# Making the low part of each fourth weight tile with an accumulating transfer in the weights-stationary projections

## The chip, the cores and the metric

One core of one Trainium2 chip runs the whole program. The metric is the device time of one execution in microseconds (us), as a median of several runs. The profile is one further execution, taken by the hardware profiler. Engines are named as the profile names them: PE is TensorE's matmul, PEld its weight load, ACT is ScalarE, DVE is VectorE, POOL is GpSimd, SP is the engine that issues the loads here.

## The reference

Two layers act on a residual stream `h` of 256 tokens by 2048 columns in float32. Each layer is `h += mixer(rms_norm(h))` and then `h += relu(rms_norm(h) @ up)^2 @ down`, with `up` 2048 by 8192 and `down` 8192 by 2048. The first mixer is a sparse attention (16 heads, 4 key heads, an indexer that keeps 64 of the keys), the second an mLSTM (8 heads). Nearly all arithmetic is the products of the stream with weights that are read once from memory, 2048 rows and 512 columns at a time.

## The kernel before, in words

To keep float32 accuracy, the kernel takes each float32 operand apart into a high part, which is its value in the type float32r, and a low part, the value minus the high part. A product of two operands is then three products of parts: high by high, high by low, low by high.

`weights()` (L138) supplies half a block of rows in two *weight tiles*. A weight tile is 256 rows by 512 columns, held as `[128, 2, 512]`, 512 KB. For each tile SP issues one load into a buffer of the tag `w` (five buffers); `split()` (L134) then makes `wh` on ACT (a copy that rounds, L135) and `wl = w - wh` on DVE (L136), each in one of four buffers. A call returns two tiles, and a projection of 2048 rows calls it four times, so it uses eight tiles.

There are two kinds of projection:

- `project()` (L151) has the activations stationary and the weights moving: twelve matmuls per weight tile, with 512 moving columns (L166 to L168). It serves the attention, the down matrix of the feed-forward part and most of the mLSTM.
- `project_t()` (L174) has the weights stationary and the activations moving. For each of the two blocks of 128 rows in a tile and each of four blocks of 128 columns it does one matmul with `wh` against the high and low parts of the activations together (512 moving columns, L191) and one with `wl` against the high part (256 moving columns, L193), so a tile is 16 matmuls. Its sums alternate between two groups of four PSUM banks, `acc` and `acx`. It serves the up matrix (32 calls, 16 in each layer) and the queries and keys of the mLSTM (4 calls).

After each `project_t()` of the feed-forward part, `evac_up()` (L457) empties the four banks: an ACT copy (L462), two DVE operations (L463, L464), and a split of the result into `hT` (L135 on ACT, L136 on DVE).

Order comes from the Tile framework: the program order, adjusted by its own simulated timeline at build time, with each engine executing its own list in order. A buffer is written again only when its readers are done. So the copy into `wh` for a tile waits for the last matmul that read the tile four earlier, and the load into `w` waits for the subtraction of the tile five earlier. POOL does masks at the start, two memsets per head group (L590), and four multiplications of the mLSTM's gate (L573); it issues no transfer.

Of the kernel before, what the change touches and what calls it, by code (L numbers as in the profile page):

```python
# [9 lines left out]
F32 = mybir.dt.float32  # L10
# [6 lines left out]
P = 128  # L17
# [20 lines left out]
def trunk_kernel(ctx: ExitStack, tc, x, norm_mix, norm_ffn, att_w_in, att_q_gain, att_k_gain,  # L38
# [18 lines left out]
        return f"{s}_{n[0]}"  # L57

    def pair(name):
        """The exact high and low parts of two blocks of 128 rows against all tokens."""  # L60
        return lp.tile([P, 2, 2, T], F32R, tag="pair", name=uid(name))

    def t2k(shape, dt=F32, name="t2k"):
# [23 lines left out]
        nc.tensor.transpose(pg[:, :32], g, ident[:32, :32])  # L87
        nc.vector.tensor_copy(gains[:, col:col + 32], pg[:, :32])

    # TensorE's clock comes up while the first loads run.  # L90
    warm = aux()
    for _ in range(8):
        nc.tensor.matmul(warm[:, :P], zero, zero, start=True, stop=True)
# [25 lines left out]
    nc.gpsimd.memset(one0[:, 1:2], 0.0)  # L119

    def rsqrt(a, cols):
        """1/sqrt of [P, cols] (in place of a tile's values), by Newton's method from a bit-level seed."""
        seed = small([P, cols], I32, "seed")
        y = small([P, cols], F32, "y")
        u = small([P, cols], F32, "u")
        nc.vector.tensor_scalar(seed, a.bitcast(I32), 1, None, op0=ALU.logical_shift_right)
        nc.vector.tensor_scalar(y.bitcast(I32), seed, -1.0, float(0x5F3759DF), op0=ALU.mult, op1=ALU.add)
        for _ in range(3):
            nc.vector.tensor_tensor(u, a, y, op=ALU.mult)
            nc.vector.scalar_tensor_tensor(u, u, -0.5, y, op0=ALU.mult, op1=ALU.mult)  # L130
            nc.vector.scalar_tensor_tensor(y, u, 1.5, y, op0=ALU.add, op1=ALU.mult)
        return y
# [2 lines left out]
        nc.scalar.copy(hi, src)  # L135
        nc.vector.tensor_tensor(lo, src, hi.bitcast(F32), op=ALU.subtract)  # L136

    def weights(src, k0, n0, width):  # L138
        """Rows k0.. (four blocks of 128) and columns n0..n0+width of a weight, as exact high and low parts."""
        parts = []  # L140
        for i in range(2):
            w = wp.tile([P, 2, 512], F32, tag="w", name=uid("w"), bufs=5)
            r0 = k0 + 256 * i
            nc.sync.dma_start(w[:, :, :width], src[r0:r0 + 256, n0:n0 + width].rearrange("(k p) f -> p k f", p=P))
            wh = wp.tile([P, 2, 512], F32R, tag="wh", name=uid("wh"), bufs=4)
            wl = wp.tile([P, 2, 512], F32R, tag="wl", name=uid("wl"), bufs=4)
            split(wh[:, :, :width], wl[:, :, :width], w[:, :, :width])
            parts.append((wh, wl))
        return parts

    def project(lhs, src, k0, n0, width, evac, before=None):  # L151
        """evac(m, psum): tokens of tile m against columns n0..n0+width. before(g) makes tiles 2g and 2g+1 of lhs."""
        acc = [pa.tile([P, 512], F32, tag="acc", name=uid("acc")) for _ in range(2)]
        nk = 2 * len(lhs)
        for g in range(nk // 4):
            if before is not None:
                before(g)
            for i, (wh, wl) in enumerate(weights(src, k0 + 512 * g, n0, width)):
                a = lhs[2 * g + i]
                for m in range(2):  # L160
                    ms = slice(m * P, (m + 1) * P)
                    o = acc[m][:, :width]
                    for j in range(2):
                        k = 4 * g + 2 * i + j
                        ah, al = a[:, 0, j, ms], a[:, 1, j, ms]
                        nc.tensor.matmul(o, ah, wh[:, j, :width], start=(k == 0), stop=False)  # L166
                        nc.tensor.matmul(o, ah, wl[:, j, :width], start=False, stop=False)  # L167
                        nc.tensor.matmul(o, al, wh[:, j, :width], start=False, stop=(k == nk - 1))  # L168
        for m in range(2):
            evac(m, acc[m][:, :width])  # L170
# [1 line left out]
    turn = [0]  # L172

    def project_t(lhs, src, n0, evac):  # L174
        """evac(b, psum): block b of 128 columns from n0 on, on the partitions, against all tokens; the product
        is the sum of the two halves of psum [128, 2, T]."""
        turn[0] ^= 1
        if turn[0]:
            acc = [pa.tile([P, 2, T], F32, tag="acc", name=uid("acc")) for _ in range(4)]
        else:  # L180
            acc = [px.tile([P, 2, T], F32, tag="aux", name=uid("acx")) for _ in range(4)]
        nk = 2 * len(lhs)
        for g in range(nk // 4):
            parts = weights(src, 512 * g, n0, 512)
            for kk in range(4):
                k = 4 * g + kk
                wh, wl = parts[kk // 2]
                a = lhs[k // 2]
                for j in range(4):
                    js = slice(j * P, (j + 1) * P)  # L190
                    nc.tensor.matmul(acc[j], wh[:, kk % 2, js], a[:, :, k % 2], start=(k == 0), stop=False,  # L191
                                     skip_group_check=True)
                    nc.tensor.matmul(acc[j][:, 1], wl[:, kk % 2, js], a[:, 0, k % 2], start=False,  # L193
                                     stop=(k == nk - 1), skip_group_check=True)
        for b in range(4):
            evac(b, acc[b])

    class Norm:
        """The stationary operand of a normed stream, without its tokens' factors; those come out of finish()."""

        def __init__(self, col):
            self.col = col
# [7 lines left out]
                                     accum_out=self.ss[:, m, c:c + 1])  # L210

        def chunk(self, c, squares=None):
            """squares: None for this chunk's own, True for those of all chunks, False for none."""
            for i in (2 * c, 2 * c + 1):
                p = aux()
                for j in range(2):
                    k = 2 * i + j
                    for m in range(2):
                        nc.tensor.transpose(p[:, j * T + m * P:j * T + (m + 1) * P],  # L219
                                            h[:, m, k * P:(k + 1) * P], ident)  # L220
                a = pair("xT")
                for j in range(2):
                    k = 2 * i + j
                    g = gains[:, self.col + k:self.col + k + 1]
                    src = p[:, j * T:(j + 1) * T]
                    nc.scalar.activation(a[:, 0, j], src, AF.Copy, scale=g)  # L226
                    nc.vector.scalar_tensor_tensor(a[:, 1, j], src, g, a[:, 0, j].bitcast(F32),
                                                   op0=ALU.mult, op1=ALU.subtract)
                self.lhs[i] = a
            for i in (range(4) if squares else (c,) if squares is None else ()):  # L230
                self.squares(i)
# [12 lines left out]
            return self  # L244

    def rope_cols(slab, v, heads, half, c0):
        """Turn the first 2*half columns of each head of v [P, 2, heads, d]."""
        rot = 2 * half
        shape = [P, 2, heads, rot]
        a = slab(shape, "ropa")  # L250
# [8 lines left out]
        nc.vector.tensor_tensor(v[:, :, :, :rot], a, b, op=ALU.add)  # L259

    def add_to_h(norm, r2=None):
        """Adds a product's columns to the stream, and hands them to the next norm."""

        def at(c):
            def evac(m, p):
# [8 lines left out]
        return at  # L274

    def slabs(pool, bufs):
        """Tiles of one phase: bufs by tag."""
        return lambda shape, name, tag=None: pool.tile(shape, F32, tag=tag or name, bufs=bufs[tag or name],
                                                       name=uid(name))

    # ---------------------------------------------------------------- attention
    def attention(nm, nxt, pool):
        slab = slabs(pool, {"v": 1, "kT": 1, "qT": 3, "hn": 3, "sq": 2, "ropa": 1, "ropb": 1, "lg": 5, "pT": 3, "sc": 4})
        lhs = nm.lhs
# [86 lines left out]
            bias.append(b)  # L371

        def heads_t(dst, gain):
            """evac of four heads of 128 columns: normed, turned and transposed into dst [P, 4, T]."""
            o = slab([P, 2, 4, DH], "hn")

            def evac(m, p):
# [71 lines left out]
            project(oT, w_ao, 0, 512 * c, 512, at(c))  # L449
        nxt.finish()  # L450

    # ---------------------------------------------------------------- feed-forward
    def ffn(nm, up, down, nxt, last=False):
        for q in range(4):
            hT = []
# [26 lines left out]
        if nxt is not None:  # L482
            nxt.finish()

    # ---------------------------------------------------------------- mLSTM
    def mlstm(nm, nxt, pool):
        slab = slabs(pool, {"go": 4, "mkT": 1, "mqT": 1, "mv": 2, "num": 2, "gT": 1, "row": 1, "et": 2, "pt": 2,
                            "mjunk": 2, "hs": 3})
# [4 lines left out]
        HD = MH * MV  # L493

        def put_o(m, c0, p, width):
            """sigmoid(o) times the heads' gain, for columns c0.. of o."""
            done = 0
            while done < width:
                c = c0 + done
# [17 lines left out]
        e = small([P, 2, MH], F32, "e")  # L517
        nc.vector.scalar_tensor_tensor(e, fg, -1.0, fg, op0=ALU.mult, op1=ALU.min)
        nc.scalar.activation(e, e, AF.Exp)
        # log(1 + e) as log(u) + (e - (u - 1)) / u, with u the rounded 1 + e.  # L520
        u = small([P, 2, MH], F32, "u1")
        ru = small([P, 2, MH], F32, "ru")
        nc.vector.tensor_scalar(u, e, 1.0, None, op0=ALU.add)
# [18 lines left out]
        nc.vector.tensor_tensor_scan(mm, cs, one0[:, 1:2].to_broadcast([MH, T]), 0.0, op0=ALU.max, op1=ALU.max)  # L542
        negm = slab([MH, T], "negm", "hs")
        nc.vector.scalar_tensor_tensor(negm, cum, -1.0, mm, op0=ALU.mult, op1=ALU.subtract)
        # Rows 0.. and 32.. of parts are the exact high and low parts of -mm; pick adds the two of one head.
        parts = pool.tile([40, T], F32R, tag="parts", bufs=1, name="parts")
        pick = cp.tile([40, MH], F32R, name="pick")
        nc.vector.tensor_tensor(pick, ident[:40, :MH], ident[:40, 32:32 + MH], op=ALU.add)
# [122 lines left out]


def _rope_table():
    """By position: [cos cos | -sin sin] of the attention's rotation, then the indexer's."""
    import numpy as np
    cols = []
    for rot in (RC, IC):
# [29 lines left out]
```

## Time and profile before

| what | value |
|---|---|
| median of 3 runs | 2126.35 us (2126.17 to 2127.8) |
| span of the profiled execution, first to last instruction | 2124.9 us |
| busy: PE, PEld | 2115.0 us, 1810.0 us |
| busy: DVE, ACT, POOL | 1242.6 us, 1010.1 us, 14.0 us |
| read from memory | 389.16 MB |

The profiled execution has no time of its own beside its span, which lies 1.45 us under the median of the runs. Busy times of different engines overlap, so they don't add up to the span; an engine that is busy for nearly all of it is the one whose work or waits the time is made of.

### The profile page before, as it was taken

Reading aid. Unit: us, or ns where it says so; the run is one execution under the profiler, and the core shown is the slowest. Engines: PE = TensorE matmul, PEld = TensorE weight load, DVE = VectorE, ACT = ScalarE, POOL = GpSimd, SP = SyncE. Lnnn points to the kernel's source line nnn. Section 1 sums busy time; section 2 is a strip of 40 time slices with the busy share of each in tenths; the row PEclk is TensorE's granted clock in tenths of the full one; section 3 lists DMA queues with packets and bytes.
Section 4 is the critical chain, followed back from the end, with each engine's and each line's share of the span. In section 5 each row is a group of like instructions: output and inputs, shape, how many; then the busy total and the mean of one; then the engine's idle time right before and its main releaser. Section 6 shows DMA issues by size and latency. Waiting matters only on the chain.

```text
span 2124.9 us, 27918 instructions
## 1 busy us (share of the span) xinstructions
PE 2115.0 (100%) x10748; PEld 1810.0 (85%) x10748; DVE 1242.6 (58%) x1866; ACT 1010.1 (48%) x1400; POOL 14.0 (1%) x20
## 2 busy tenths in 40 slices
PE   9999999999999999999999999999999999999999
PEld 8988888888888888888999888888888888888887
DVE  5697656645555565565654565656555555654654
ACT  6556554534443443444554554545434434443542
POOL 0000000000000000000011000000000000000000
PEclk9999999999999999999999999999999999999999
DMA  7665356656656656665566555466566666666664
GB/s 234 188 180 151 119 178 188 188 193 191 191 191 187 198 189 196 190 189 188 166 185 209 171 165 176 161 188 188 193 194 189 191 194 189 191 193 191 189 205 140
DMA packets 207926, 393.09 MB, mean 185 GB/s; under 512 B 12784, under 2 KB 29616, under 8 KB 207792
## 3 DMA queue, kind: packets, MB, share of 16 engines
q1 hardware_dynamic: 207744, 391.29, 60.4%
q8 instruction: 84, 1.38, 0.2%
q14 instruction: 50, 0.41, 0.1%
q10 hardware_dynamic: 48, 0.02, 0.0%
HBM read 389.16 MB, written 2.10 MB: 184 GB/s over the span
## 4 chain that ended last, share of the span: by engine, by line
PE 99%; ACT 0%; DMA 0%; DVE 0%; issue 0%; SPq 0%; DVEq 0%
PE acc L167 19%; PE acc L168 19%; PE acc L166 19%; PE acc L191 13%; PE acx L191 13%; PE acc L193 6%; PE acx L193 6%; PE aux L219 1%; PE aux L412 0%; PE aux L440 0%; PE aux L620 0%; PE aux L349 0%; DMA w<-in_att_w_in_dram 0%; PE aux L611 0%; PE aux L396 0%; PE aux L645 0%
## 5 line engine op out<-in xcount | busy, mean ns | idle before, releaser
L136 DVE TENSOR_TENSOR wl<-w,wh 128x1024 fp32r<-128x1024 f32 (+3 forms) x752 | 907.1, 1207 | 820.6 <-ACT wh L135 819.5
L135 ACT CAST wh<-w 128x1024 fp32r<-128x1024 f32 (+3 forms) x752 | 777.6, 1035 | 970.6 <-PE acc L168 576.6
L191 PE MATMUL acc<-xT,wh 128*128 128x512 f32 x1152 | 401.1, 394 | 0.0
L191 PE MATMUL acx<-xT,wh 128*128 128x512 f32 x1152 | 399.9, 393 | 0.0
L166 PE MATMUL acc<-wh,hT 128*128 128x512 f32 x1024 | 398.7, 389 | 0.0
L167 PE MATMUL acc<-wl,hT 128*128 128x512 f32 x1024 | 398.7, 389 | 0.0
L168 PE MATMUL acc<-wh,hT 128*128 128x512 f32 x1024 | 398.4, 389 | 0.0
L193 PE MATMUL acc<-xT,wl 128*128 128x256 f32 x1152 | 318.9, 278 | 0.0
L193 PE MATMUL acx<-xT,wl 128*128 128x256 f32 x1152 | 318.4, 278 | 0.0
L191 PEld LDWEIGHTS acx<-xT,wh 128*128 128x128 f32 x1152 | 215.7, 187 | 49.3
L191 PEld LDWEIGHTS acc<-xT,wh 128*128 128x128 f32 x1152 | 215.4, 188 | 48.9
L166 PEld LDWEIGHTS acc<-wh,hT 128*128 128x128 f32 x1024 | 192.2, 188 | 40.0
L168 PEld LDWEIGHTS acc<-wh,hT 128*128 128x128 f32 x1024 | 192.2, 188 | 39.7
L167 PEld LDWEIGHTS acc<-wl,hT 128*128 128x128 f32 x1024 | 192.2, 188 | 39.5
L193 PEld LDWEIGHTS acc<-xT,wl 128*128 128x128 f32 x1152 | 216.5, 188 | 1.3
L193 PEld LDWEIGHTS acx<-xT,wl 128*128 128x128 f32 x1152 | 216.2, 188 | 0.3
L166 PE MATMUL acc<-wh,xT 128*128 128x512 f32 (+3 forms) x576 | 212.4, 372 | 2.3 <-ACT xT L226 2.3
L167 PE MATMUL acc<-wl,xT 128*128 128x512 f32 (+3 forms) x576 | 212.7, 371 | 0.0
L168 PE MATMUL acc<-wh,xT 128*128 128x512 f32 (+3 forms) x576 | 211.9, 371 | 0.0
L166 PEld LDWEIGHTS acc<-wh,xT 128*128 128x128 f32 x576 | 108.1, 188 | 15.1 <-ACT xT L226 2.5
L167 PEld LDWEIGHTS acc<-wl,xT 128*128 128x128 f32 x576 | 108.3, 188 | 12.9 <-issue 0.7
L168 PEld LDWEIGHTS acc<-wh,xT 128*128 128x128 f32 x576 | 108.3, 188 | 12.8 <-issue 0.3
(204 smaller groups left out, 1308.1 us busy)
## 6 DMA issues: line engine op xcount, KB each, us to landing
w<-in_ffn_w_up_dram SPq DMA_DIRECT2D x256, 512.0 KB, 3.8
w<-in_ffn_w_down_dram SPq DMA_DIRECT2D x256, 512.0 KB, 4.3
w<-in_ml_w_in_dram SPq DMA_DIRECT2D x64, 512.0 KB, 3.8
w<-in_att_w_in_dram SPq DMA_DIRECT2D x48, 512.0 KB, 4.4
w<-in_att_w_out_dram SPq DMA_DIRECT2D x32, 512.0 KB, 4.4
w<-in_ml_w_out_dram SPq DMA_DIRECT2D x32, 512.0 KB, 3.7
w<-in_ml_w_in_dram SPq DMA_DIRECT2D x32, 412.0 KB, 3.7
w<-in_att_w_in_dram SPq DMA_DIRECT2D x24, 368.0 KB, 3.6
```

The source lines that it names most:

```text
L135: nc.scalar.copy(hi, src)
L136: nc.vector.tensor_tensor(lo, src, hi.bitcast(F32), op=ALU.subtract)
L166: nc.tensor.matmul(o, ah, wh[:, j, :width], start=(k == 0), stop=False)
L167: nc.tensor.matmul(o, ah, wl[:, j, :width], start=False, stop=False)
L168: nc.tensor.matmul(o, al, wh[:, j, :width], start=False, stop=(k == nk - 1))
L191: nc.tensor.matmul(acc[j], wh[:, kk % 2, js], a[:, :, k % 2], start=(k == 0), stop=False, skip_group_check=True)
L193: nc.tensor.matmul(acc[j][:, 1], wl[:, kk % 2, js], a[:, 0, k % 2], start=False, stop=(k == nk - 1), skip_group_check=True)
L219: nc.tensor.transpose(p[:, j * T + m * P:j * T + (m + 1) * P], h[:, m, k * P:(k + 1) * P], ident)
```

## The change

`weights()` gets a flag `moved` and counts the tiles that it has made, over the whole program. `project_t()` sets the flag. Where the flag is set and the count is a multiple of four, the tile's parts are made in another way: ACT writes `wh` as before, then ACT writes `-wh` into `wl`, and then a transfer issued by POOL adds `w` onto `wl` in place. The other tiles keep the old way. As every projection uses eight tiles, the fourth and the eighth tile of each `project_t()` are the ones that change. The diff also takes out docstrings and comments, which are left out here (their lines are kept empty, so line numbers below L138 move by the added lines alone).

```diff
+    tiles = [0]
+
-    def weights(src, k0, n0, width):
+    def weights(src, k0, n0, width, moved=False):
...
             wh = wp.tile([P, 2, 512], F32R, tag="wh", name=uid("wh"), bufs=4)
             wl = wp.tile([P, 2, 512], F32R, tag="wl", name=uid("wl"), bufs=4)
-            split(wh[:, :, :width], wl[:, :, :width], w[:, :, :width])
+            tiles[0] += 1
+            if moved and tiles[0] % 4 == 0:
+                nc.scalar.copy(wh, w)
+                nc.scalar.activation(wl, wh.bitcast(F32), AF.Copy, scale=-1.0)
+                nc.gpsimd.dma_start(wl, w, accum_op=ALU.add)
+            else:
+                split(wh[:, :, :width], wl[:, :, :width], w[:, :, :width])
             parts.append((wh, wl))
...
     def project_t(lhs, src, n0, evac):
...
-            parts = weights(src, 512 * g, n0, 512)
+            parts = weights(src, 512 * g, n0, 512, True)
```

## Rows read from the trace of the kernel before

**Rows 1.** The page, span and busy time of each engine.

```profile
span 2124.9 us, 27918 instructions
...
PE 2115.0 (100%) x10748; PEld 1810.0 (85%) x10748; DVE 1242.6 (58%) x1866; ACT 1010.1 (48%) x1400; POOL 14.0 (1%) x20
```

**Rows 2.** The page, the chain that ended last, shares by engine.

```profile
PE 99%; ACT 0%; DMA 0%; DVE 0%; issue 0%; SPq 0%; DVEq 0%
```

**Rows 3.** Groups by line and shape: count, busy us, mean ns, idle before, releaser.

```profile
L136 DVE TENSOR_TENSOR wl<-w,wh 128x1024 fp32r<-128x1024 f32 x688 | 842.5, 1225 | 759.6 <-ACT wh L135 759.1
L135 ACT CAST wh<-w 128x1024 fp32r<-128x1024 f32 x688 | 723.2, 1052 | 907.8 <-PE acc L168 521.1 <-PE acc L191 180.9 <-PE acx L191 167.6
...
L193 PE MATMUL acc<-xT,wl 128*128 128x256 f32 x1152 | 318.9, 278 | 0.0
L193 PE MATMUL acx<-xT,wl 128*128 128x256 f32 x1152 | 318.4, 278 | 0.0
```

**Rows 4.** Tile wl: who waited for the instructions that make or read it.

```profile
  PEld acc L167: 0.6, 1
  PE acc L167: 0.4, 1
```

**Rows 5.** Timeline of ACT, 348 to 370 us: start, duration, instruction, idle before.

```profile
350.13 1.05 ACT L135 CAST wh<-w 128x1024 fp32r<-128x1024 f32 x1
351.08 0.38 ACT L462 COPY u<-acc 128x256 f32<-128x256 f32 x1
351.34 1.03 ACT L135 CAST hT<-u 128x256 fp32r<-128x256 f32 x3
352.91 1.06 ACT L135 CAST wh<-w 128x1024 fp32r<-128x1024 f32 x1 [0.54 <-ACT hT L135]
354.53 0.41 ACT L135 CAST hT<-u 128x256 fp32r<-128x256 f32 x1 [0.56 <-DVE u L464]
355.68 1.05 ACT L135 CAST wh<-w 128x1024 fp32r<-128x1024 f32 x1 [0.75 <-PE acx L191]
358.46 1.05 ACT L135 CAST wh<-w 128x1024 fp32r<-128x1024 f32 x1 [1.72 <-PE acx L191]
361.23 1.05 ACT L135 CAST wh<-w 128x1024 fp32r<-128x1024 f32 x1 [1.72 <-PE acx L191]
363.96 1.05 ACT L135 CAST wh<-w 128x1024 fp32r<-128x1024 f32 x1 [1.68 <-PE acx L191]
366.73 1.05 ACT L135 CAST wh<-w 128x1024 fp32r<-128x1024 f32 x1 [1.72 <-PE acx L191]
369.51 1.05 ACT L135 CAST wh<-w 128x1024 fp32r<-128x1024 f32 x1 [1.72 <-PE acx L191]
```

**Rows 6.** Tile w: its loads, and the time from issue to landing.

```profile
L144 SPq DMA_DIRECT2D w<-in_ffn_w_up_dram x256: 367/368/368, 306.7 to 2011.1; - x128
...
DMA to landing us min/median/max: 3.1/3.8/8.5
```

**Rows 7.** Busy by stretch (PE, PEld, DVE, ACT, POOL), clock, DMA share, GB/s.

```profile
0.00:5.00 5.00, 3.95 (x17) 3.67 (x17) 0.56 (x2) 2.01 (x3) 1.96 (x12) 1.00 0.61 159
5.00:10.00 5.00, 2.73 (x14) 2.13 (x14) 1.67 (x3) 3.27 (x6) 0.00 (x0) 0.96 1.03 348
10.00:15.00 5.00, 5.00 (x20) 4.16 (x20) 3.88 (x8) 4.41 (x12) 0.00 (x0) 0.70 1.05 393
...
327.00:416.00 89.00, 89.00 (x518) 77.86 (x517) 55.35 (x89) 44.43 (x65) 0.00 (x0) 1.00 0.63 188
```

**Rows 8.** Timeline of POOL, 1100 to 1250 us.

```profile
1107.49 5.71 POOL L573 TENSOR_TENSOR go<-go,hg 128x1024 f32<-128x1024 f32 x2 [837.85 <-ACT go L502]
1125.73 5.97 POOL L573 TENSOR_TENSOR go<-go,hg 128x1024 f32<-128x1024 f32 x2 [12.53 <-ACT go L502]
1210.31 0.10 POOL L590 MEMSET mv<- 128x8 f32 x1 [78.62 <-PE aux L622]
1239.27 0.11 POOL L590 MEMSET mv<- 128x8 f32 x1 [28.85 <-PE aux L622]
```

**Rows 9.** Timeline of ACT, 1120 to 1133 us, in the mLSTM.

```profile
1126.66 1.05 ACT L135 CAST wh<-w 128x1024 fp32r<-128x1024 f32 x1
```

**Rows 10.** Waits of SP's queue: us in total, times, longest.

```profile
SPq L144 <- DVE wl L136: 1317.9, 577, 9.1
```

## The prediction, made before the change was run

> **What bounds the kernel now.** I read the page first. PE is busy 2115.0 of 2124.9 us, and PE is 99% of the chain that ended last [rows 1, 2]. All the time that PE is idle comes to 2124.9 - 2115.0 = 9.9 us; that is the most that any change which leaves the matmuls alone could give back. DVE is busy 1242.6 us [rows 1], and its largest group is the one that the change thins out, the subtraction into `wl` at 1225 ns each [rows 3]. But nobody is kept by it: all that PE waited for `wl` in the whole execution is two waits of 0.6 and 0.4 us [rows 4], and DVE itself sits idle 759 us before this group, waiting for ACT's copy [rows 3]. ACT's copy in turn waits for PE to let go of a buffer: its idle time ends with a matmul, L168 or L191 [rows 3]. So PE sets the pace, ACT and DVE follow it, and what matters of the change is how late it makes `wl`, not how much work it takes from DVE.
>
> **How late may wl be?** The timeline of ACT gives it [rows 5]. In `project_t()` the copies into `wh` start 2.73 to 2.78 us apart (361.23, 363.96, 366.73, 369.51), which is PE's time for one tile. The copy at 361.23 waited for the last matmul with `wh` of the tile four earlier. Three tiles lie between that and the tile's own first matmul, and the third copy after it, at 369.51, is the one that waits for the last `wh` matmul of the tile just before. So PE asks for the new tile at about 369.51, 8.3 us after its copy began. By the old way `wl` is ready 1.05 + 1.23 = 2.3 us after that start, so about 6 us are spare. The change spends from these 8.3 us.
>
> **The change part by part.**
>
> *How many.* The two groups of L193 are 2304 matmuls [rows 3], eight per tile: 288 tiles in 36 calls, of which each fourth changes, 72: 36 fourth tiles and 36 eighth ones.
>
> *Removed.* 72 subtractions of 1.225 us, 88 us of DVE [rows 3]. DVE is on no path, so this is worth 0 us; its cover is PE, and without that cover the gain could still not exceed the 9.9 us above.
>
> *ACT's second pass.* 72 more passes over 128x1024, taken at the copy's 1.05 us [rows 3], 76 us of ACT. For an eighth tile the copy starts as the one at 361.23, with 1.68 us idle behind it [rows 5]: the negation fits there and ends 2.1 us after the copy's start. The copy for a fourth tile starts as the call before is emptied, like the one at 350.13 [rows 5]: a copy of 0.38 us and three `hT` copies of 1.03 us stand right behind it, and are older in the program. The negation ends 2.3 us after the copy's start if only the first goes ahead, 3.3 us if all do; I take 2.8. The next weight copies have 0.5 to 0.75 us of idle before them there and some 6 us of spare behind, so their delay costs 0.
>
> *The transfer.* Its issue by POOL and its adding are nowhere in this trace, so I bound it. From below: a load of the same 512 KB takes 3.8 us from issue to landing [rows 6]. From above: the longest landing of such a load, 8.5 us [rows 6], with POOL held as long as by its longest kind of instruction, 5.71/2 = 2.9 us [rows 8], 11.4 us. Between them: DMA is busy 0.63 of the stretch from 327 to 416 us [rows 7], 0.63 x 2.77 = 1.75 us for each load, the rest of the 3.8 being fixed. An add must read two operands, `w` and `wl`, so I add 1.75 to get 5.55 us, and for POOL to write the transfer's list, which no row shows, half of the 2.9: 7.05 us. This is nearer to the load, because the transfer is one of the same size between the same kinds of rows. A rule of the Trainium skill speaks for less: "DMA: Bandwidth & Descriptors", section "Anatomy of one DMA — SWDGE (gpsimd) path", gives a transfer issued by GpSimd about 2.0 us plus its bytes at 436 GB/s. For one pass over 512 KB that is 3.2 us, for two 4.4 us, and the stalls summed below would be 0. Another speaks for the doubling: "Collectives: The Full Stack", section "The bandwidth ceiling: the fold count and why AG ≠ RS ≠ AR", says that an add in a transfer costs by its two source reads, not by its arithmetic. No run shows either here.
>
> *The stall.* For an eighth tile 2.1 + 7.05 - 8.3 = 0.85 us, for a fourth one 2.8 + 7.05 - 8.3 = 1.55 us. These don't hide each other: the next changed tile's copy waits for this tile's matmuls, so each has its own 8.3 us. The sum is 36 x (0.85 + 1.55) = 86 us.
>
> *What is queued behind.* POOL: the change's transfers stand in line with L573. In the mLSTM the copy for the first changed tile starts at 1126.66 [rows 9], its transfer wants to go at about 1129, and POOL is held until 1125.73 + 5.97 = 1131.7 [rows 8]: about 3 us, once. The memsets at 1210 and 1239 [rows 8] are 0.1 us; if one stands ahead of a transfer while waiting for its buffer, it costs a few us once, which I leave out. SP: a load waits now for the subtraction five tiles back [rows 10]; after the change each fourth one waits for the transfer, and the loads behind it with it. With 7.05 us it goes out 9.15 us after the copy's start and lands at 12.95; its copy is due five tiles on, at 13.85. This is hidden, barely, with 6 us of spare behind.
>
> **The sum.** Span 2124.9 + 86 + 3 = 2214 us, and with the 1.45 us that the median lies above the span 2215 us.
>
> **The rivals.**
>
> *A. The transfer is quick and nothing changes.* With a transfer of up to 8.3 - 2.8 = 5.5 us every `wl` is there in time. For it speak the 3.8 us of a load [rows 6] and that the data does not come from memory but from the chip; against it, that the landing must contain one read more, and POOL's share. The time is 2126 us, perhaps 3 more for the mLSTM's one wait. It decides at 5.5 us of transfer. The page on DMA named above is on its side.
>
> *B. The transfer is dear.* At the upper bound, 11.4 us, the stalls are 5.2 and 5.9 us, 36 x 11.1 = 400 us, 2529 us. For it: nothing in the trace shows POOL issuing a transfer quickly, and it shares DMA engines that are at 0.63 [rows 7]. Such gaps can also cost clock: in the first 15 us PE was busy 2.73 of 5 us and the granted clock in the next 5 us was 0.70, a mean between the levels 1.2 and 2.4 GHz [rows 7]. Forecast stalls leave PE busy about nine tenths, so I count nothing for that; here a third of the time is gap, and it could come on top.
>
> *C. The DMA engines become the bound.* In 11.1 us (four tiles) the loads leave (1 - 0.63) x 11.1 = 4.1 us of the engines [rows 7]. A doubled load takes 3.5 of that. If adding runs at a lower rate and takes 6 us of them, each period grows by 1.9 us whatever the latency: 72 x 1.9 = 137 us, 2263 us. It decides from 4.1 us on.
>
> *D. Faster.* DVE, or the order of instructions, gives back part of the 9.9 us. Nothing in the waits on `wl` (1.0 us) speaks for it.
>
> **How the numbers follow.** What a measurement can tell from no change is 0.2%, 4.3 us. Forecast, stalls of a fraction of a us to about 3 us per changed tile: 0.40. A: 0.27. B: 0.20. C: 0.10. D: 0.03. So faster 0.03, same 0.27, slower 0.70. The range begins at A, 2123 us, and reaches into B as far as a transfer of 10.3 us, where the stalls are 4.1 and 4.8 us, 36 x 8.9 = 320 us, 2449 us; it leaves out the far half of B and part of D. The forecast's own range goes from 5.7 us of transfer (2126 + 36 x 0.2 = 2133) to 9 us (36 x (2.8 + 3.5) = 227, 2356), 2133 to 2356 us.
>
> **What would show it.** In the profile after: PE waits at L193 for a transfer into `wl`, 72 times, longer at fourth than at eighth tiles; the transfer's time to landing, near 7 us; DVE down by some 88 us and ACT up by some 76; the idle time of PE grown by about what the span grew. Step by step: if PE does not wait and landing is under 5.5 us, A; if landing is over 10 us, B; if DMA shares are near 1 in the stages of `project_t()` and the copies into `wh` wait for loads, C. The prediction is wrong if the spare 8.3 us is not what it seems (copies that start later, or PE asking earlier), or if the framework sets PE's matmuls with `wl` later and so hides the transfer.

## The result and the profile after

| | before | after |
|---|---|---|
| median of the runs | 2126.41 us (2126.17 to 2127.8, 4 runs) | 2141.75 us (2140.48 to 2143.02, 4 runs) |
| span of the profiled execution | 2124.9 us [rows 1] | 2141.2 us |

The ratio is 1.007, with a 95% interval from 1.0056 to 1.0084. The kernel became slower, by 15.3 us or 0.7%, where 89 us were forecast. The page after, span and busy times:

```profile
span 2141.2 us, 28137 instructions
...
PE 2129.8 (99%) x10748; PEld 1817.1 (85%) x10748; DVE 1162.8 (54%) x1794; ACT 1079.2 (50%) x1472; POOL 74.6 (3%) x92
...
q0 software_dynamic: 10368, 37.75, 9.8%
```

PE's busy time grew by 14.8 us and the span by 16.3, though PE issues the same 10748 matmuls. So nearly all the loss is not idle time of PE: the matmuls themselves stand further apart. The groups by line and shape after, and then the line of the transfers, L153, with who waited for it and its time to landing:

```profile
L136 DVE TENSOR_TENSOR wl<-w,wh 128x1024 fp32r<-128x1024 f32 x616 | 753.9, 1224 | 829.7 <-ACT wh L135 829.3
...
L152 ACT ACTIVATE wl<-wh 128x1024 fp32r<-128x1024 f32 x72 | 76.3, 1060 | 1.4
...
L201 PE MATMUL acc<-xT,wl 128*128 128x256 f32 x1152 | 305.3, 281 | 0.2 <-DMA wl<-w 0.2
```

```profile
L153 POOL DMA_DIRECT2D wl<-w x72: 841/857/993, 333.2 to 2041.1; - x72
...
who waited for it (us, times):
  PEld acx L201: 0.7, 1
  PEld acc L201: 0.6, 1
  PE acx L201: 0.3, 1
  PE acc L201: 0.2, 1
...
DMA to landing us min/median/max: 4.5/4.8/9.5
```

A transfer holds POOL 0.86 us and lands 4.8 us after its issue, in the median. Of the 72 transfers two were waited for. At each of the two both PE and its weight load PEld are listed, which overlap, so the four rows are not four waits: PE itself stood idle 0.2 + 0.3 = 0.5 us. The stalls that the forecast was made of are not there. One eighth tile shows both sides, first on the timelines of ACT and POOL, then on that of PE (start, duration, instruction, idle before):

```profile
696.32 1.05 ACT L151 CAST wh<-w 128x1024 fp32r<-128x1024 f32 x1 [1.79 <-PE acc L199]
697.40 1.06 ACT L152 ACTIVATE wl<-wh 128x1024 fp32r<-128x1024 f32 x1
```

```profile
698.76 0.85 POOL L153 DMA_DIRECT2D wl<-w  x1 [10.25 <-ACT wl L152]
```

```profile
703.15 0.28 PE L201 MATMUL acc<-xT,wl 128*128 128x256 f32 x1
703.26 0.40 PE L199 MATMUL acc<-xT,wh 128*128 128x512 f32 x1
...
704.32 0.40 PE L199 MATMUL acc<-xT,wh 128*128 128x512 f32 x1
704.56 0.28 PE L201 MATMUL acc<-xT,wl 128*128 128x256 f32 x1
704.67 1.11 PE L199 MATMUL acc<-xT,wh 128*128 128x512 f32 x4
705.62 0.39 PE L199 MATMUL acx<-xT,wh 128*128 128x512 f32 x1
705.85 0.64 PE L201 MATMUL acc<-xT,wl 128*128 128x256 f32 x4
```

With 4.8 us the transfer issued at 698.76 lands at about 703.6. PE comes to the tile at 704.67. But it no longer alternates there. In what follows a *long* matmul is one with `wh` (512 moving columns, L199, formerly L191), a *short* one is one with `wl` (256, L201, formerly L193), and a *pair* is a long one and its short one. At 704.67 stand four long ones, then the next call's first long one (into `acx`), and only then the four short ones. That is the order in which the program was built, not a wait on the chip. At a fourth tile there are four long ones and then four short ones:

```profile
693.39 1.08 PE L199 MATMUL acc<-xT,wh 128*128 128x512 f32 x4
694.31 0.64 PE L201 MATMUL acc<-xT,wl 128*128 128x256 f32 x4
```

Such a *place* stands at 69 of the 72 changed tiles: 44 with four long and four short, and 25 with the next call's long one ahead as well. The three other tiles are among the mLSTM's calls, which have two more places of four and four that stand in the kernel before too. The framework put the 69 there because of the transfer: built with DVE's addition in the transfer's place and nothing else changed, the program alternates again at these tiles, as in the kernel before.

The loss lies between these places. Beside the rows of PE above, from 703.26 to 704.32 (three pairs in 1.06 us), stand three pairs of the kernel before, which take 1.04 us (700.00 to 701.04):

```profile
700.00 0.39 PE L191 MATMUL acc<-xT,wh 128*128 128x512 f32 x1
700.24 0.27 PE L193 MATMUL acc<-xT,wl 128*128 128x256 f32 x1
...
701.04 0.40 PE L191 MATMUL acc<-xT,wh 128*128 128x512 f32 x1
```

I timed three pairs in strict turn, start to start, from every long matmul of `project_t()` on. Before, 2079 of 2235 such stretches take 1.035 to 1.046 us (the *quick pace*) and 95 take 1.057 to 1.072 us (the *slow pace*). After, 137 are quick and 1470 slow. At full size the difference is 2304 pairs [rows 3], 768 stretches of three, by 0.02 us: 15 us. A whole stage of the up matrix, four of which lie in a layer, shows it: from the first long to the last short matmul 679.49 to 768.18 before, 88.69 us, and 90.34 us after (first the two ends before, then the two after):

```profile
679.49 0.39 PE L191 MATMUL acc<-xT,wh 128*128 128x512 f32 x1
...
768.18 0.27 PE L193 MATMUL acx<-xT,wl 128*128 128x256 f32 x1
```

```profile
685.02 0.39 PE L199 MATMUL acc<-xT,wh 128*128 128x512 f32 x1
...
775.36 0.28 PE L201 MATMUL acx<-xT,wl 128*128 128x256 f32 x1
```

The rest is small. The stretch between two such stages is 0.17 us shorter than before, so that eight stages lose 8 x 1.48 = 11.8 us; the mLSTM loses 1.8 us; and 2.6 us are lost before the first `project_t()`, where the granted clock of the profiled execution fell from 2.4 to 1.2 GHz twice, so that its mean over a stretch is 0.52 and 0.66 (busy by stretch, then clock, DMA share and GB/s; the first two and the last answer to [rows 7]). In the stretch before the first fall PE was busy 1.68 of 5 us.

```profile
5.00:10.00 5.00, 1.68 (x10) 1.19 (x9) 1.14 (x2) 2.80 (x6) 0.00 (x0) 0.79 0.99 337
10.00:15.00 5.00, 5.00 (x17) 3.79 (x16) 3.70 (x8) 3.79 (x10) 0.00 (x0) 0.52 1.04 386
236.00:241.00 5.00, 4.25 (x17) 3.64 (x18) 1.57 (x4) 1.90 (x6) 0.00 (x0) 0.66 0.65 201
329.50:418.50 89.00, 89.00 (x509) 77.40 (x508) 45.64 (x80) 51.15 (x72) 6.94 (x8) 1.00 0.81 227
```

The 2.6 us before the first `project_t()` are not the change's, which alters nothing there. order4 (below), which has no transfer, shows the same two falls of the clock in its profile and comes to its first `project_t()` at 329.7 us, after at 329.5, before with one fall at 326.9, and nohoist with none at 324.6. The executions of most kernels here, the one before too, fall into spans some 2 to 3 us apart by the mean clock: the kernel before takes 2123.8 to 2125.7 us at a mean clock of 0.999 and 2125.8 to 2128.1 at 0.998. The table below therefore has the span at 0.999 beside the ratio.

### The profile page after: what moved, and what is told of

It reads as the page before. It is cut to its first block, busy times and chain, and to the rows that moved or that the text cites. A ratio compares the mean times of both kernels' runs of the same rounds, so it can differ in the third digit from the quotient of the medians.

```text
span 2141.2 us, 28137 instructions
## 1 busy us (share of the span) xinstructions
PE 2129.8 (99%) x10748; PEld 1817.1 (85%) x10748; DVE 1162.8 (54%) x1794; ACT 1079.2 (50%) x1472; POOL 74.6 (3%) x92
## 5 line engine op out<-in xcount | busy, mean ns | idle before, releaser
L136 DVE TENSOR_TENSOR wl<-w,wh 128x1024 fp32r<-128x1024 f32 (+3 forms) x680 | 818.5, 1205 | 890.8 <-ACT wh L135 889.7
L135 ACT CAST wh<-w 128x1024 fp32r<-128x1024 f32 (+3 forms) x680 | 701.9, 1033 | 843.0 <-PE acc L176 562.5
L199 PE MATMUL acc<-xT,wh 128*128 128x512 f32 x1152 | 396.3, 398 | 0.0
L199 PE MATMUL acx<-xT,wh 128*128 128x512 f32 x1152 | 396.3, 398 | 0.0
L201 PE MATMUL acc<-xT,wl 128*128 128x256 f32 x1152 | 305.3, 281 | 0.2 <-DMA wl<-w 0.2
L201 PE MATMUL acx<-xT,wl 128*128 128x256 f32 x1152 | 305.1, 281 | 0.3 <-DMA wl<-w 0.3
L199 PEld LDWEIGHTS acx<-xT,wh 128*128 128x128 f32 x1152 | 214.0, 188 | 49.2
L199 PEld LDWEIGHTS acc<-xT,wh 128*128 128x128 f32 x1152 | 213.6, 188 | 48.4
L201 PEld LDWEIGHTS acc<-xT,wl 128*128 128x128 f32 x1152 | 212.6, 189 | 5.0 <-DMA wl<-w 0.6
L201 PEld LDWEIGHTS acx<-xT,wl 128*128 128x128 f32 x1152 | 212.2, 189 | 4.6 <-DMA wl<-w 0.7
```

## Experiments

Three theories. **O**: the order of PE's matmuls costs the time. **T**: the transfers' traffic slows PE down. **W**: PE waits for the transfers, or for what they delay. O alone makes the time depend on the order when there is no transfer.

| run | transfers | places changed | ratio, 95% interval | span at clock 0.999, us | stretches quick / slow |
|---|---|---|---|---|---|
| before | 0 | none | 1 | 2123.8 to 2125.7 | 2079 / 95 |
| after | 72 | 71 | 1.007 (1.0056 to 1.0084) | 2138.7 to 2139.1 | 137 / 1470 |
| order4 | 0 | 73, four and four | 1.0035 (1.0022 to 1.0047) | 2131.6 to 2132.2 | 749 / 966 |
| order2 | 0 | 72, two and two | 1.0031 (1.0019 to 1.0042) | 2130.8 to 2132.1 | 903 / 985 |
| order4all | 0 | every block, four and four | 1.0039 (1.0024 to 1.0054) | 2132.8 | none alternates |
| pinned | 72 | none | 1.0016 (1.0007 to 1.0025) | 2127.9 to 2130.2 | 1738 / 406 |
| hoist | 0 | 73, as after | 1.0052 (1.004 to 1.0065) | 2137.1 to 2137.7 | 173 / 1422 |
| nohoist | 72 | 71, four and four | 1.0035 (1.0022 to 1.0047) | 2133.0 to 2133.2 | 750 / 982 |
| negate | 0 | none | 1.0004 (0.9995 to 1.0013) | 2125.4 to 2126.8 | 2069 / 118 |
| twice2 | 0 | 144, two and two | 1.006 (1.0047 to 1.0072) | 2137.7 | 120 / 1498 |
| shift2 | 0 | 144, two and two | 1.002 (1.0011 to 1.0029) | 2128.7 to 2129.5 | 1210 / 426 |
| shift1 | 0 | 144, two and two | 1.0019 (1.001 to 1.0027) | 2127.9 to 2129.4 | 1263 / 367 |
| order2all | 0 | every block, two and two | 1.0015 (1.0006 to 1.0023) | 2127.7 to 2128.7 | none alternates |

(71 and 73 hold the two places of four and four of the mLSTM that stand in the kernel before too; 72 and 144 are what the edits set. A few further places at the starts of calls are irregular in all, the kernel before among them. A span at 0.999 is of one to seven executions; that of the kernel before is of many.)

**order4 and order4all: the order without the transfers.** The kernel before, with the old split; only the loop of `project_t()` over the four blocks of columns runs in another order in the first row block of each fourth and eighth tile (order4) or in every row block (order4all).

```diff
+ALT = [(j, low) for j in range(4) for low in (0, 1)]
+FOUR = [(j, low) for low in (0, 1) for j in range(4)]
...
-                for j in range(4):
+                for j, low in (FOUR if g % 2 and kk == 2 else ALT):
...
+                    if not low:
                         nc.tensor.matmul(acc[j], wh[:, kk % 2, js], ...
+                    else:
                         nc.tensor.matmul(acc[j][:, 1], wl[:, kk % 2, js], ...
```

> The kernel before with nothing changed but the order of eight matmuls at each fourth and eighth weight tile of project_t: in the tile's first block the four matmuls with wh come first and then the four with wl, the order that the trace of the changed kernel shows on PE. No transfer is added, DVE makes every wl. Theory O (order: PE itself runs slower after such a place, because its alternation of long and short matmuls falls into a slower pace, 1060 ns per six matmuls where before it is 1040): 2137 to 2143 us, and the slow pace is seen behind every such place. Theory T (the transfers and ACT's second pass slow PE's reads): 2126 us. Theory W (PE waits for late transfers): 2126 us.

> The kernel before with four long matmuls and then four short ones in every block of project_t, 576 places in place of 72. Theory O in the form that each place costs by itself (0.2 us each): some 2126 + 115 = 2240 us. In the form of a pace that is set: no more than the slow pace everywhere, 2304 pairs x 6.7 ns = 15 us, so 2135 to 2145 us, or less if long matmuls in a row run at the 227 ns that project shows. Theories T and W: 2126 us.

Measured: 2135.55 us against 2127.33 of the kernel before for order4, and 2136.94 for order4all. The order alone costs about 8 us, half of the loss, with no transfer in the program. Eight times as many places cost hardly more: it is not a price for each place. order4 came out between the theories, under the 2137 us of O and over the 2126 us of T and W: within it the pace changes at each place, slow behind one and quick behind the next, and not slow behind every one as O expected.

**order2: a smaller disorder.** As order4, with two long and two short matmuls and then two pairs in that row block.

```diff
+TWO = [(0, 0), (1, 0), (0, 1), (1, 1)] + ALT[4:]
...
-                for j in range(4):
+                for j, low in (TWO if g % 2 and kk == 2 else ALT):
```

> As the order-only kernel, but only two long matmuls, then two short ones, at the same 72 places; the kernel before has this pattern once at the start of most stages, and the fast pace follows it. Theory O in the form that the pace is a state which the place sets: 2125 to 2129 us. Theory O in the form that each irregular place or each run of like matmuls costs by itself: some 2130 to 2134 us, between before and the four-and-four kernel. Theories T and W: 2126 us.

Measured: 2134.25 us, the same as order4 within the intervals, though only two matmuls trade places. The pace again alternates from place to place. The time lies at the upper edge of the 2130 to 2134 us expected if each place costs, but a pace that alternates is against a fixed cost; the 2125 to 2129 us of a place that sets the quick pace were missed.

**pinned: the transfers without the order.** The changed kernel, with dependencies that hold PE's old order and bring no semaphore.

```diff
+                    if last[0] is not None and (g % 2 and kk > 1 or k == 0 and j == 0):
+                        tc.add_manual_dep(hi.ins, last[0].name, nosync, reason="order")
+                    last[0] = lo.ins
```

> The changed kernel, all 72 transfers kept, with extra ordering edges on PE that bring its matmuls back to the strict alternation of the kernel before. Theory O: 2124 to 2129 us, pace 1040 ns per six matmuls. Theory T: 2138 to 2143 us with a slow pace in spite of the order. Theory W: 2142 us or more, since without the four long matmuls that now go ahead PE asks for wl up to 0.7 us earlier, and waits before L201-like matmuls grow to 72 x 0.2 us and more.

Measured: 2131.2 us, ratio 1.0016. This lies between O's 2129 and T's 2138 us. The 72 transfers land in 4.5 to 6.0 us, 4.8 in the median. Even with the old order the profile lists a wait at only two of the 72 tiles: at one PE stands idle 0.9 us (and PEld over the same time), at the other PEld alone waits 0.2 us (the line of the transfers, who waited and time to landing, then the two waits):

```profile
  PEld acc L203: 1.4, 2
  PE acc L203: 0.9, 1
...
DMA to landing us min/median/max: 4.5/4.8/6.0
```

```profile
1135.43 0.38 PE L203 MATMUL acc<-xT,wl 128*128 128x256 f32 x1 [0.88 <-DMA wl<-w]
```

```profile
1966.69 0.19 PEld L203 LDWEIGHTS acc<-xT,wl 128*128 128x128 f32 x1 [0.20 <-DMA wl<-w]
```

So T and W together account for at most a few us. What is left shows where it sits: six up stages keep the quick pace (each 0.95 us longer than before by the order at its ends, and the stretch behind it 0.87 us shorter, so +0.08), the mLSTM loses 1.2 us, and the last two up stages, which lose the quick pace in spells, 2.4 us. In the very last, one stretch of three pairs takes 1.20 us, and the 63 behind it are slow to the stage's end; in the one before it, 31 slow stretches end behind one of 1.15 us. So a delay of 0.1 to 0.2 us, far too short to count as a stall, can turn the pace either way. All three turns of these spells fall where a transfer lands just as PE comes to its tile: the landings are at 1789.78, 1823.86 and 1966.65, and PE's weight load from the tile starts within 0.05 us of each. They are the three transfers of the up stages with the least time to spare before the tile's first short matmul (0.04 to 0.23 us; the next has 0.34). The second and third are the delays of 0.1 to 0.2 us; at the first no wait shows.

**negate: ACT's second pass alone.** As pinned, with DVE adding in the transfer's place.

```diff
-                nc.gpsimd.dma_start(wl, w, accum_op=ALU.add)
+                nc.vector.tensor_tensor(wl, w, wl.bitcast(F32), op=ALU.add)
```

> ACT's second pass kept and the old matmul order held, but the addition onto the negated part made by DVE and no transfer. If what is left with the old order (some 4 us) comes from waits for transfers or from their traffic: as the kernel before, 2125 to 2128 us, fast pace. If it comes from ACT's second pass and the delays that it gives to ACT's other work: 2129 to 2132 us.

Measured: 2128.78 us, ratio 1.0004, not to be told from the kernel before, with the quick pace. (The median lies between the two figures expected.) ACT's 76 us more are hidden, as forecast; what pinned costs beyond this comes with the transfers.

**hoist and nohoist: the two kinds of place.** hoist is order4 and, in 24 of the eighth tiles, the next call's first long matmul ahead of the four short ones, which gives PE nearly the changed kernel's order without a transfer. nohoist is the changed kernel with that one matmul held back, transfers and four-and-four places kept.

```diff
+                        if k == 0 and j == 0:
+                            for lo in last if col[0] == n0 and n0 % 2048 else []:
+                                tc.add_manual_dep(lo, hi.ins.name, nosync, reason="order")
+                            last.clear()
```

```diff
+                    if last[0] is not None and k == 0 and j == 0:
+                        tc.add_manual_dep(hi.ins, last[0].name, nosync, reason="order")
+                    last[0] = lo.ins
```

> The old split, no transfer, but the matmul order of the changed kernel: four long then four short in the first block of each changed tile, and in 24 of the eighth tiles the next call's first long matmul ahead of the short ones. If the order makes the whole loss: 2139 to 2143 us, the feed-forward up stage near 90.3 us, and the slow pace (1060 ns per six matmuls) nearly everywhere, as in the changed kernel. If the order with transfers counts apart (order some 8 us, transfers some 4, the rest a mixture): 2134 to 2137 us, stage near 89.6 us, slow and fast pace by turns.

> The changed kernel with its transfers and its four long and four short matmuls, but with the next call's first long matmul held back behind the call before it: 71 places of four and four, no other. If only the order counts: as the old split with that order, 2134 to 2137 us. If the transfers cost some 4 us besides, as they did with the old order: 2138 to 2141 us. If the call's long matmul that goes ahead is the harmful part, the pace is by turns slow and fast here; if the transfers hold the slow pace, it is slow nearly everywhere.

Measured: hoist 2139.46 us against 2127.24, nohoist 2135.02. hoist gives 12.2 of the 15.3 us without one transfer, and its pace is slow nearly everywhere, as in the changed kernel: with the next call's matmul ahead in each second place, the pace does not turn back there as it does in order4 and nohoist. Adding the transfers at an equal order costs 1.2 us (nohoist against the middle of order4's 2131.6 to 2132.2) and 1.5 us (after against hoist), by the middles of the spans at 0.999, of two or three executions each. The expectation that pinned's 4 us would add to any order failed.

**twice2: two places in each tile.** If a place turned the pace over, whatever its surroundings, the second would undo the first. The edit is order2's, in both row blocks of the tile.

```diff
+                for j, low in (TWO if g % 2 and kk >= 2 else ALT):
```

> The old split, no transfer, and two irregular places (two long, two short) in each of the 72 tiles instead of one, some 2.8/2 us apart. If a place turns the pace from fast to slow or back, so that the second undoes the first: close to the kernel before, 2126 to 2130 us, with the fast pace in most windows. If each place costs a fixed amount: twice the loss with one place per tile, some 14 us, 2140 to 2143 us. If the pace is slow in some share of the time whatever the count: 2133 to 2136 us.

Measured: 2139.8 us, slow nearly everywhere. The simple turning-over is wrong: a second place that follows three pairs behind the first did not bring the quick pace back. Its 2139.8 us lie at the edge of what a fixed price for each place would give, but order4all's 576 places are against such a price. On the timeline of PE (two-and-two places are the x2 rows; three pairs from 518.42 on take 1.06 us, and again from 519.48):

```profile
516.31 0.62 PE L195 MATMUL acc<-xT,wh 128*128 128x512 f32 x2
516.78 0.40 PE L198 MATMUL acc<-xT,wl 128*128 128x256 f32 x2
...
517.72 0.62 PE L195 MATMUL acc<-xT,wh 128*128 128x512 f32 x2
518.18 0.40 PE L198 MATMUL acc<-xT,wl 128*128 128x256 f32 x2
518.42 0.40 PE L195 MATMUL acc<-xT,wh 128*128 128x512 f32 x1
...
519.48 0.40 PE L195 MATMUL acc<-xT,wh 128*128 128x512 f32 x1
...
520.54 0.40 PE L195 MATMUL acc<-xT,wh 128*128 128x512 f32 x1
```

The starts in the trace gave the next theory. In the quick pace the spacings of matmuls repeat after two pairs (231, 112, 233, 117 ns), in the slow pace after three (233, 117, 241, 120, 236, 113 ns). The pairs between two places are counted from the last short matmul of one to the first long one of the next, both included. Behind a place the slow pace had ended where 31 pairs (order2) or 29 (order4) lay between, and had stayed where 3 or 27 did (twice2), which are multiples of its period. So what a place does would depend on where in the period it falls.

**shift2 and shift1: the same places, moved.** The second place of the tile stands two columns of blocks later (5 and 25 pairs between places, shift2) or one (4 and 26, shift1).

```diff
+LATE = ALT[:4] + [(2, 0), (3, 0), (2, 1), (3, 1)]                    # shift2
+LATE = ALT[:2] + [(1, 0), (2, 0), (1, 1), (2, 1)] + ALT[6:]          # shift1
...
+                for j, low in ((TWO, LATE)[kk - 2] if g % 2 and kk >= 2 else ALT):
```

> Again 144 places of two long and two short matmuls, two in each of the 72 tiles, but the second one two columns of blocks later, so that 5 and then 25 regular pairs lie between places, where 3 and then 27 lay. If a place turns the pace by the phase in which it falls (so far: out of the slow pace, whose spacings repeat after three pairs, behind 31 and 29 pairs but not behind 3 or 27; out of the fast pace, whose spacings repeat after two, behind 31 and 29): slow for the 5 pairs only, fast for the 25, so 2127 to 2131 us with the fast pace in most windows. If it is the number of places or their kind that costs: 2139 to 2142 us as with 3 and 27.

> The same with the second place one column of blocks later: 4 and then 26 regular pairs between places. By the phase, the second place leaves the slow pace behind 4 pairs; the next first place then falls behind 26 pairs of the fast pace, an even number, which no run has shown: either it stays fast there too and the pace is then turned by the next ones at 4 and 26 in some regular manner, anywhere from 2128 to 2138 us. If the number of places costs: 2139 to 2142 us.

Measured: 2132.84 and 2131.18 us against 2127.76, where twice2 lost 12.6. The same number of places of the same kind, the second one or two positions later, costs 0.3 to 0.4 of that. shift2's median lies 2 us above what was expected, but its pace does what the theory said (timeline of PE: a place at 514.87, the slow 1.06 us from 515.57 to 516.63, a place at 516.98, and behind it the quick 1.04 us from 517.69 to 518.73, which holds for the 25 pairs):

```profile
514.87 0.62 PE L196 MATMUL acc<-xT,wh 128*128 128x512 f32 x2
515.33 0.40 PE L199 MATMUL acc<-xT,wl 128*128 128x256 f32 x2
515.57 0.40 PE L196 MATMUL acc<-xT,wh 128*128 128x512 f32 x1
...
516.63 0.40 PE L196 MATMUL acc<-xT,wh 128*128 128x512 f32 x1
...
516.98 0.64 PE L196 MATMUL acc<-xT,wh 128*128 128x512 f32 x2
517.45 0.40 PE L199 MATMUL acc<-xT,wl 128*128 128x256 f32 x2
517.69 0.39 PE L196 MATMUL acc<-xT,wh 128*128 128x512 f32 x1
...
518.73 0.39 PE L196 MATMUL acc<-xT,wh 128*128 128x512 f32 x1
```

In the up stages looked at, each place that came in the quick pace (behind 31, 29, 26 or 25 pairs, and the first of a stage behind 15) brought the slow one. The kernel before has one turn of this kind too: each of its eight up stages starts in the slow pace and goes over to the quick one at its single place of two and two, eight pairs on.

**order2all: another regular order.** Two long and two short in turn, everywhere.

> Two long and two short matmuls in turn in every block of the old split, so that the order is regular again, with another pattern. No theory gives its pace; if irregular places are what costs, a regular order should be near the kernel before, 2125 to 2129 us; if alternation itself is the cheap one, as the run with four and four everywhere suggests, 2134 to 2140 us.

Measured: 2130.56 us, ratio 1.0015: between the two figures expected, better than four and four, a little worse than strict turn. No order tried beats that of the kernel before, and no kernel here beats it.

## Why the prediction was wrong

**What bounds the kernel, and what would be free: right.** PE is still busy 99% of the span. DVE lost 72 subtractions and 842.5 - 753.9 = 88.6 us of them [rows 3], forecast 88, for nothing. (The two waits of [rows 4] are one, of PE and its weight load at the same moment.) ACT gained 76.3 us, forecast 76, and negate showed that these cost nothing that can be told.

**The 8.3 us until PE asks for `wl`: right.** In the eighth tile shown, the copy starts at 696.32 and PE reaches the tile at 704.67, 8.35 us later; over the 36 eighth tiles the median is 8.35 us too, over the fourth ones 8.1. The negations end 2.14 and 2.6 us after the copy's start in the median, forecast 2.1 and 2.8; POOL begins the issue 0.3 us later, which the sum left out.

**The transfer: 7.05 us forecast, 4.8 us measured.** This is the term that failed. (By its own parts it should read 5.55 + 1.45 = 7.0 us, and the stalls 83 us and not 86.) Both additions to the load's 3.8 us [rows 6] were too large. POOL's part was taken as half of 2.9 us and is 0.86. What remains, 4.8 - 0.86 = 3.9 us, is about a plain load's landing: the second operand's 1.75 us does not appear in it. In the time of the DMA engines it does appear, 2.9 us for each transfer (below) against the 1.75 reckoned for a load. Why the landing does not grow by as much stays open: the transfer also reads from the chip and not from memory, and no run here has a plain transfer within the chip. Put into the forecast's own sum, 2.8 + 4.8 = 7.6 and 2.1 + 4.8 = 6.9 us both stay under 8.3, so the 86 us of stalls go to nothing, and pinned, which keeps the order for which that sum was made, shows one idle time of PE of 0.9 us and one wait of PEld of 0.2. The figure that the prediction gave beside the sum, from the Trainium skill, "DMA: Bandwidth & Descriptors", section "Anatomy of one DMA — SWDGE (gpsimd) path", was an estimate of 3.2 us for one pass over the bytes and 4.4 for two; the traces come out a little above the second.

**The rivals.** A had the mechanism of the transfer (4.8 us, under its 5.5) and not the time, 2126 to 2129 us. That the time lies within the forecast's own range, 2133 to 2356 us, and that the kernel became slower as forecast, is luck: the stalls that the range was made of are not there. B is excluded by the landing. C's threshold, 4.1 us of the DMA engines per transfer, was not reached: the queue's 9.8% of the span over 72 transfers is 2.9 us each, and the stage's share went from 0.63 [rows 7] to 0.81. D did not happen.

**POOL in the mLSTM: right in place, smaller in price.** POOL is in its last multiplication of the gate as forecast and issues the transfer as that ends; PE then idles 0.21 us of the 3 forecast. In pinned, where no four long matmuls go ahead, it is 0.88 us (1135.43, above): the forecast's 3 us stood on a transfer that had used up all of the 8.3 us.

```profile
1134.21 4.98 POOL L581 TENSOR_TENSOR go<-go,hg 128x1024 f32<-128x1024 f32 x2 [12.53 <-ACT go L510]
1139.14 0.86 POOL L153 DMA_DIRECT2D wl<-w  x1
```

```profile
1142.70 1.09 PE L199 MATMUL acc<-xT,wh 128*128 128x512 f32 x4
1144.00 0.39 PE L201 MATMUL acc<-xT,wl 128*128 128x256 f32 x1 [0.21 <-DMA wl<-w]
```

**What the sum had no term for.** The prediction named, as what would make it wrong, that the framework might set the matmuls with `wl` later and so hide the transfer. It did that, at nearly every changed tile, but the prediction counted such an order as free. It was not needed (pinned) and is the larger part of the loss: hoist, with that order and no transfer, lies 12.2 us over the kernel before, out of 15.3. The other 3 us are settled in part. About half goes with the clock of the first 330 us, since at equal clock the spans of the two differ by 1.5. By the profiles, from the first `project_t()` on, the changed kernel loses 13.7 us and hoist 12.0; of the 1.7 between them 1.4 lie in the mLSTM, where the two waits stand. PE's idle time at these waits is 0.5 us, so the rest stays open. Why a disturbed order leaves PE at 1060 ns for three pairs instead of 1040 stays open: the runs show when the slow pace begins and ends, not what in PE keeps it.

## What to carry to other kernels

When a change makes an operand come later, compare the order in which the framework builds the engine that sets the time, before and after; a reorder that hides a wait which would not have come can cost more than the wait. A kernel bound by PE with no idle time can still lose through the spacing of its matmuls: look at start-to-start times of a repeating group, not only at waits. Here a transfer inside the chip cost a load's landing and its measured issue; test such a price with the order held before believing stalls.

## What the hardware showed that was not expected

Matmuls of 512 and 256 moving columns in strict turn, at a granted clock of 1.00, run at either of two paces, 1040 or 1060 ns for three pairs, and keep it for a whole stage until something disturbs them. Two matmuls that trade places, or one delay of 0.16 us, are enough to go from the quick to the slow pace. In the runs a place of two and two or four and four led back out of the slow pace behind 4, 5, 29 and 31 pairs and not behind 3 or 27, multiples of the slow pace's three-pair repeat; 144 such places cost 12.6 us at the one spacing and 3.4 to 5.1 us at the others.

A transfer of 512 KB that adds onto its target within the chip landed in the median in 4.8 us, of which 0.86 us hold POOL. The remaining 3.9 us are about the landing of a plain load of the same size from memory (3.8 us before; 4.2 for the loads of the up matrix after). Of the DMA engines' time it took 2.9 us, where the prediction reckoned 1.75 for a load.
